# Stick-breaking attention moved from head order to token-tile order, beside the output projection and the FFN

## The chip, the cores and the metric

One core of a Trainium2 chip runs one launch of the kernel. The core has five engines with a queue each: PE (TensorE, matrix multiplication, with its weight loads as PEld), DVE (VectorE), ACT (ScalarE), POOL (GpSimd) and SP, which here issues every DMA. The metric is device time in microseconds (us) of the whole launch; lower is better.

## The reference, cut to what matters

One decoder layer over 2048 positions of width 1024, all in float32:

```python
h = rmsnorm(x, attn_pre_norm)
dq, dk, dv, sq, sk, sv = split(h @ w_qkv)            # 1024 -> 3072
diff_o = rmsnorm(diff_attention(dq, dk, dv))          # 4 heads, two softmax maps of 64, values of 128
# stick-breaking attention, 8 heads of 64, strictly causal
z = sq @ sk.T / 8
log_1mb = where(strict, log_sigmoid(-z), 0)
between = cumsum(log_1mb, reverse) - log_1mb
a = where(strict, exp(log_sigmoid(z) + between), 0)
sb_o = rmsnorm(a @ sv)
x = x + rmsnorm(concat(diff_o, sb_o) @ w_o)
h = rmsnorm(x, ffn_pre_norm)
u = causal_conv3(h @ w_up) + conv_b                   # 1024 -> 2 * 2816
x = x + rmsnorm((gelu(gate) * val) @ w_down)          # 2816 -> 1024
```

## The kernel before, in words

Every float32 operand of a matmul is split into a high part, rounded to the matmul's own type fp32r, and a low part, the rest; each product is three matmuls: high by high, high by low, low by high. So each operand costs a copy ("hi") and a subtraction ("lo") on ACT, DVE or POOL, and PE gets three passes.

The program doesn't run in the order of its loops. Each step of the loops registers its operations with a planner (class `Plan`): engine, estimated cost, dependencies, buffers, and a due time that is the running sum of PE cost in the order of registration (`plan.now`), less a lead. `Plan.run` then plays the operations through, gives each engine at each moment the ready operation that is due first, lets some operations go to either of two engines (`alt`), and writes the instructions out in that order. On the chip each engine works through its own list in order and waits on semaphores. `merge(a, b)` mixes two streams of steps so that both go forward in proportion to their PE cost.

Five kinds of work follow each other, with overlap:

- **QKV.** Five passes over eight blocks of 256 positions (`qkv_steps`, `unit_steps`): 128x256 matmuls into banks `g` (L602, L605), results split and stored to DRAM.
- **Differential attention**, heads 0 to 3 (`diff_stream`), mixed with the passes: logits `z` (L702), softmax on DVE and ACT, 128x128 transposes through PE into banks `t` (L720), a hi copy (L466 or L467) and a lo subtraction (L734), values into bank `o` (L905 to L911).
- **Stick-breaking attention**, heads 4 to 7, two 64-wide maps each (`sb_stream`), after it in head order, 256 positions at a time: per map, per key chunk of up to 512 and per block of 128 queries one `z` (L702), two sigmoids on ACT out of `z` (L969, L971), a running product along the row on DVE (the scan, L977), a product on POOL (L982), then the transposes, hi, lo and two value matmuls (L1000). `fin_sb` normalises, and `mix_out` stores the result. It runs beside the last QKV passes and the first eight blocks of the output projection.
- **Output projection** (`wo_block`, L1101), one block of 128 positions at a time, then residual, second norm and a store of the transposed FFN input (`h2d`).
- **FFN** (`ffn_all`), four tiles of 512 positions: 44 `up` blocks of 24 matmuls (L1226), per block a copy out of PSUM (L1234), two halo copies and three conv operations (L1232, L1235, L1238 to L1240), gelu on ACT (L1243), the product (L1248) and its split (L1249, L1250); then `down` (L1311), two halves of 22 row blocks by four banks. Each weight block (512 KB) is loaded from the input and split again in each of the four tiles (L458, L461, L459). The FFN holds eight PSUM banks.

What sets the due times of attention and FFN is the order at the end of `layer_kernel`:

```python
heads = chain(diff_stream(seq, 32), sb_stream(seq, 32, 2))
...
run(merge(until(heads, *mark), qkv_steps(p, i0, i1)))     # 15 marks
wo_weights()
run(until(heads, 7, 5))
run(merge(until(heads), chain.from_iterable(wo_block(b) for b in range(8))))
for b in range(8, NB):
    run(wo_block(b))
ffn_all()
plan.run()
```

## Time and profile before

| | |
|---|---|
| median of 3 runs | 3088.07 us (3087.9 to 3089.95) |
| the profiled execution, its own time | 3094.23 us |
| span of its instructions | 3092.5 us |
| PE, DVE, ACT, POOL busy in the span | 97%, 73%, 47%, 31% |
| granted TensorE clock, mean | 0.992 of 2.4 GHz |
| instructions on PE (matmul) | 17352 |

The trace holds every instruction with start, duration and tiles. Matmuls are pipelined: one of 512 columns is shown with some 390 ns, while the next starts after some 227 ns. So a busy share of PE is no measure of how densely it is fed; the distance from start to start is. Times in the rows are us from the start of the span, unless ns is said.

### The profile page before, as it was taken

How to read it: one execution, taken by the hardware profiler on the slowest of the kernel's cores; microseconds unless marked ns; L12 is line 12 of the kernel's file. 1: busy time of each engine (PE TensorE's matmuls, PEld its weight loads, DVE VectorE, ACT ScalarE, POOL GpSimd, SP SyncE). 2: the span in 40 equal slices, each digit the busy share in tenths (PEclk: the TensorE clock that was granted, in tenths of full speed). 3: DMA queues.
4: the chain of work that ended last, by engine and by line, in shares of the span. 5: the costliest groups of instructions: out<-in, count | busy, mean ns of one | idle time of the engine just before them, and what ended most of it. 6: DMA issues, size and time to landing. Idle time of an engine off the chain costs nothing. (4 is left out here: it accounts for less than half of the span.)

```text
span 3092.5 us, 48117 instructions
## 1 busy us (share of the span) xinstructions
PE 2984.5 (97%) x17352; PEld 2610.4 (84%) x17352; DVE 2252.0 (73%) x4327; ACT 1442.9 (47%) x2913; POOL 951.6 (31%) x1047
## 2 busy tenths in 40 slices
PE   7999999999999999889999999999999999999998
PEld 7899999999888888868877888888888888888887
DVE  4658878897999999998754864387744776277742
ACT  4434545555777767666643433233322433233321
POOL 1001002002766777675411211033301332023310
PEclk9999999999999999999999999999999999999999
DMA  8776656655634366533363333443344333343332
GB/s 264 246 209 186 185 151 201 171 156 159 188 122 130 95 194 185 151 100 112 110 214 126 102 100 116 121 134 96 96 129 143 96 99 106 119 141 101 96 123 82
DMA packets 392146, 437.11 MB, mean 141 GB/s; under 512 B 20096, under 2 KB 328164, under 8 KB 381668
## 3 DMA queue, kind: packets, MB, share of 16 engines
q1 hardware_dynamic: 391908, 434.05, 46.7%
q8 instruction: 136, 2.23, 0.3%
q14 instruction: 102, 0.84, 0.1%
HBM read 333.30 MB, written 100.67 MB: 140 GB/s over the span
## 5 line engine op out<-in xcount | busy, mean ns | idle before, releaser
L1226 PE MATMUL pu<-fh,fhi 128*128 128x512 f32 x2816 | 869.0, 390 | 0.2 <-ACT fu L1234 0.2
L1226 PEld LDWEIGHTS pu<-fh,fhi 128*128 128x128 f32 x2816 | 529.4, 188 | 110.5 <-ACT fu L1234 0.6
L461 DVE TENSOR_TENSOR flo<-fraw,fhi 128x1024 fp32r<-128x1024 f32 x186 | 233.0, 1254 | 488.6 <-ACT fhi L458 488.5
L1226 PE MATMUL pu<-fh,flo 128*128 128x512 f32 x1408 | 549.2, 390 | 0.0
L982 POOL TENSOR_TENSOR ring_w<-ring_w,ring_a 128x512 f32<-128x512 f32 (+2 forms) x320 | 387.9, 1224 | 220.3 <-DVE ring_a L977 121.1
L605 PE MATMUL g<-hT,big 128*128 128x256 f32 x3072 | 447.8, 288 | 7.3 <-DVE st L638 4.3
L458 ACT CAST fhi<-fraw 128x1024 fp32r<-128x1024 f32 x253 | 265.5, 1051 | 397.4 <-PE py L1311 218.6
L1311 PE MATMUL py<-fhi,gt 128*128 128x512 f32 x1408 | 435.9, 390 | 0.0
L605 PEld LDWEIGHTS g<-hT,big 128*128 128x128 f32 x3072 | 405.4, 192 | 19.8 <-DVE st L638 4.4
L977 DVE TENSOR_TENSOR_SCAN ring_a<-ring_a 128x513 f32<-128x513 f32 (+2 forms) x320 | 412.8, 1316 | 6.1 <-ACT ring_a L969 6.1
L702 PE MATMUL z<-k,q 128*128 128x512 f32 (+3 forms) x1280 | 362.5, 376 | 10.4 <-ACT ring_a L969 7.0
L466 ACT CAST thi<-t 128x512 fp32r<-128x512 f32 (+2 forms) x472 | 221.6, 492 | 210.1 <-PE t L720 179.3
L1311 PEld LDWEIGHTS py<-fhi,gt 128*128 128x128 f32 x1408 | 264.5, 188 | 60.0
L1226 PEld LDWEIGHTS pu<-fh,flo 128*128 128x128 f32 x1408 | 264.7, 188 | 54.9
L734 DVE TENSOR_TENSOR tlo<-t,thi 128x512 fp32r<-128x512 f32 (+2 forms) x528 | 281.6, 556 | 34.6 <-ACT thi L466 28.4
L459 POOL TENSOR_TENSOR flo<-fraw,fhi 128x1024 fp32r<-128x1024 f32 x78 | 195.8, 2510 | 338.9 <-DVE fhi L457 171.2
L1311 PE MATMUL py<-flo,gt 128*128 128x512 f32 x704 | 277.8, 395 | 0.0
L720 PE MATMUL t<-ident,ring_w 128*128 128x128 f32 x1632 | 253.2, 276 | 22.4 <-DVE tlo L734 18.5
L1250 POOL TENSOR_TENSOR gt<-fy,gt 128x512 fp32r<-128x512 f32 x88 | 118.4, 1347 | 493.9 <-ACT gt L1249 483.0
L1239 DVE SCALAR_TENSOR_TENSOR fy<-fu,cw,fy 128x512 f32<-128x512 f32 x176 | 239.6, 1361 | 6.2
L384 POOL TENSOR_TENSOR sm<-sm,neghalf 128x2 f32<-128x2 f32 (+1 forms) x72 | 76.8, 1067 | 536.5 <-DVE sm L382 534.7
L602 PE MATMUL g<-big,hT 128*128 128x256 f32 x1536 | 227.4, 288 | 6.3 <-DVE st L624 1.5
(158 smaller groups left out, 4697.4 us busy)
## 6 DMA issues: line engine op xcount, KB each, us to landing
fraw<-in_w_up_dram SPq DMA_DIRECT2D x176, 512.0 KB, 3.8
hT<-hd SPq DMA_DIRECT2D x64, 1024.0 KB, 7.0
fraw<-in_w_down_dram SPq DMA_DIRECT2D x88, 512.0 KB, 3.8
q<-qd SPq DMA_DIRECT2D x128, 256.0 KB, 4.3
hd<-hT SPq DMA_DIRECT2D x16, 1024.0 KB, 5.4
qd<-st SPq DMA_DIRECT2D x128, 128.0 KB, 2.6
kd<-st SPq DMA_DIRECT2D x128, 128.0 KB, 2.6
vd<-st SPq DMA_DIRECT2D x64, 256.0 KB, 5.2
```

The source lines that it names most:

```text
L458: "ACT", c_act(n) + 42, lambda: nc.scalar.copy(hi(), raw()))
L461: "DVE", c_dvs(n), lambda: nc.vector.tensor_tensor(lo(), raw(), f32(hi()), ALU.subtract))
L602: nc.tensor.matmul(ps.t[:, cs], hk[:, b, c * P:(c + 1) * P], wv[:, a, k, :], start=first, stop=last)
L605: nc.tensor.matmul(ps.t[:, cs], wv[:, a, k, c * P:(c + 1) * P], hk[:, b, :], start=first, stop=last)
L702: nc.tensor.matmul(ps.t[:, 0:w], q.t[:, m, l, jj * P:(jj + 1) * P], kt.t[:, m, 0:w], start=(l == 0), stop=(l == 1 and not masked))
L720: nc.tensor.transpose(ps.t[:, cc * P:(cc + 1) * P], rows[jj].t[:, (k + kk) * P:(k + kk + 1) * P], ident)
L734: ol = op("DVE", c_dvp(n), lambda sl=sl: nc.vector.tensor_tensor(lo.t[:, sl], ps.t[:, sl], f32(hi.t[:, sl]), ALU.subtract), (oh,), (ps, hi ...
L977: nc.vector.tensor_tensor_scan(gr, gr, gr, 1.0 if cb is None else cb[0].t[:, 0:1], ALU.mult, ALU.bypass)
L982: rdeps.append(op("POOL", c_pool(w), lambda be=be, gm=gm, w=w: nc.gpsimd.tensor_tensor(be.t, be.t, gm.t[:, 1:w + 1], ALU.mult), (o1, o2), ...
L1226: nc.tensor.matmul(ps.t, w3(w)[:, k, :], h.t[:, a, k, :], start=(k == 0 and i == 0), stop=(k == KD - 1 and i == 2))
L1239: nc.vector.scalar_tensor_tensor(y.t, u.t[:, 1:TT + 1], cw[:, 1, f:f + 1], y.t, ALU.mult, ALU.add)
L1311: nc.tensor.matmul(ps.t, gt.t[:, a, j * P:(j + 1) * P], wt.t[:, ms], start=(m == 0 and i == 0), stop=(m == NFT - 1 and i == 2))
```

## The change

Nothing of the arithmetic's volume on PE changes. What is done where and when does:

- The planner's matmul cost becomes n * 0.4434 ns, and it knows of a 1300 ns cost when ACT's function changes between `sig` and `gelu` (`table`); it adds that cost to the operation it has picked, and doesn't pick by it.
- Only the four differential heads stay in the first stage, with three and a half of now four QKV passes. Then `sb_open` replaces the left pools, and stick-breaking attention runs by token tiles of 512: tile, then head, map, key chunk from the diagonal down. PSUM: two banks `z2`, one `t2`, one `o2`, and four banks `pf` that projection and FFN share (eight in all).
- The output projection (`wo`) works on a tile of 512. Its input is stored already split (`mixd` holds hi and lo, the norm's gain applied in `mix_out`), and loads straight into matmul operands. The FFN input `h2` is made in SBUF and no longer goes through DRAM.
- Weights are loaded and split once, in pieces of half the size, and the split form is stored to DRAM (`wud`, `wdd`, `wod`); the other three tiles load the split form. Five buffers `W`, in strict order of use.
- FFN in rounds: `up` for 6, 6, 6 and 4 row blocks, each followed by `down` over those, on four banks; partial sums are kept in SBUF (`ya`) and added by DVE.
- The conv takes its first term, scale and bias, on ACT out of PSUM, and two shifted terms on DVE out of PSUM; two short `edge` operations add the halo.

```diff
-    heads = chain(diff_stream(seq, 32), sb_stream(seq, 32, 2))
+    heads = diff_stream(seq, len(seq))
...
-    wo_weights()
-    run(until(heads, 7, 5))
-    run(merge(until(heads), chain.from_iterable(wo_block(b) for b in range(8))))
-    for b in range(8, NB):
-        run(wo_block(b))
-    ffn_all()
+    for mark, p, i0, i1 in (((0, 2), 0, 4, 6), ((0, 4), 0, 6, 8), ((1, 4), 1, 0, 4), ((2, 0), 1, 4, 8),
+                            ((2, 6), 2, 0, 4), ((3, 4), 2, 4, 8), ((), 3, 0, 4)):
         run(merge(until(heads, *mark), qkv_steps(p, i0, i1)))
+    op(None, 0, sb_open, users("k", "v", "q", "thi", "tlo", "mo", "ot", "os", "sq", "mix", "sm", "z", "o", "w", "a"))
+    sb = sb_stream()
+    run(merge(until(sb, 1, 2), qkv_steps(3, 4, 8)))
+    ffn_switch()
+    run(merge(until(sb, 1, 5), wo(0)))
+    run(merge(until(sb, 1, 8), h2(0)))
+    head = list(ffn_head(2))
+    run(merge(until(sb), chain(ffn(0), ffn(1), head[:-5])))
+    run(chain(head[-5:], ffn_tail(2), ffn(3)))
     plan.run()
```

The order inside the FFN, the weights, and the new steps of an `up` block:

```diff
+    ROUNDS = ((0, 6), (6, 12), (12, 18), (18, NFT))
+    def ffn_head(t):
+        for r, (a, b) in enumerate(ROUNDS):
+            for m in range(a, b):
+                for v in range(2):
+                    yield 24 * c_mm(512), lambda m=m, v=v: up(t, m, v)
+            if r + 1 < len(ROUNDS):
+                for h in range(2):
+                    yield from down(t, r, h)
+    def ffn_tail(t):
+        if t + 1 < NTT:
+            yield from wo(t + 1)
+        for h in range(2):
+            yield from down(t, len(ROUNDS) - 1, h)
+        if t + 1 < NTT:
+            yield from h2(t + 1)
...
+    def weight(n):
+        kind, a, b = key = jobs[n]
+        w = buf("W")
+        if key in wstore:
+            wbufs[n] = w, (load(flat, home, 1 << 19, (w,), (wstore[key],), lead=0.0, what="wload"),)
+            return
+        raw = buf("raw2")
...
+        o = load(rv, src, 1 << 18, (raw,), lead=0.0, what="wraw")
+        ds = split(lambda: raw.t, lambda: w.t[:, 0, :], lambda: w.t[:, 1, :], 512, (o,), (raw, w), 0.0)
+        wstore[key] = op(SPE, 0, lambda: nc.sync.dma_start(home, flat()), ds, (w,), 0, 1 << 19, "wstore")
...
+        o1 = op("ACT", c_act(512) + 95, lambda: nc.scalar.activation(
+            y.t, ps.t, AF.Identity, scale=sc(2), bias=sc(3)), (last, *mem["cw"]), (ps, y), what="conv")
+        def conv():
+            nc.vector.scalar_tensor_tensor(y.t[:, 1:TT], ps.t[:, 0:TT - 1], sc(1), y.t[:, 1:TT], ALU.mult, ALU.add)
+            nc.vector.scalar_tensor_tensor(y.t[:, 2:TT], ps.t[:, 0:TT - 2], sc(0), y.t[:, 2:TT], ALU.mult, ALU.add)
...
+            o = op("ACT", 520, lambda: nc.scalar.activation(y.t, y.t, AF.Gelu_apprx_tanh), (o,), (y,)).table("gelu")
```

One unit of the new stick-breaking stream (a map, a key chunk of 512, four query blocks `jj`), its front and one of its four transposing steps:

```diff
+            o = op("PE", 2 * c_mm(w) + (60 if diag else 0), z, [*ql, kl, mem["masks"]], (ps, q, kt), what="z")
+            o1 = op("ACT", c_act(w), lambda: nc.scalar.activation(
+                gm.t[:, 0:w], ps.t[:, 0:w], AF.Sigmoid, scale=-1.0), (o,), (gm, ps), what="sig").table("sig")
+            o2 = op("ACT", c_act(w), lambda: nc.scalar.activation(
+                be.t[:, 0:w], ps.t[:, 0:w], AF.Sigmoid), (o,), (be, ps), what="sig").table("sig")
...
+            o1 = op("DVE", c_scan(w), scan, [o0, o1] + ([cb[1]] if cb else []), [gm] + ([cb[0]] if cb else []),
+                    what="scan")
+            carry[jj] = gm, o1
+            o = op("POOL", c_pool(w), lambda: nc.gpsimd.tensor_tensor(
+                be.t[:, 0:w], be.t[:, 0:w], gm.t[:, 1:w + 1], ALU.mult), (o1, o2), (be, gm), what="mul").alt(
...
+            oh = copy(lambda: hi.t[:, sl], lambda: ps.t[:, sl], n, (o,), (ps, hi), "hi")
+            ol = op("DVE", c_dvp(n), lambda: nc.vector.tensor_tensor(
+                lo.t[:, sl], ps.t[:, sl], f32(hi.t[:, sl]), ALU.subtract), (oh,), (ps, hi, lo), what="lo")
             if pend:
                 av(*pend.popleft())
```

## Rows read from the trace of the kernel before

**Rows 1.** The page, busy time, share of the span, instructions of an engine.

```profile
PE 2984.5 (97%) x17352; PEld 2610.4 (84%) x17352; DVE 2252.0 (73%) x4327; ACT 1442.9 (47%) x2913; POOL 951.6 (31%) x1047
```

**Rows 2.** Busy time of each engine by stretch, clock, DMA share, GB/s.

```profile
core 0: us, PE busy (x) PEld busy (x) DVE busy (x) ACT busy (x) POOL busy (x), PEclk, DMA share, GB/s
0.00:100.00 100.00, 77.89 (x583) 74.21 (x584) 46.67 (x104) 37.77 (x85) 14.60 (x23) 0.97 0.84 267
100.00:800.00 700.00, 690.33 (x5307) 659.60 (x5306) 571.58 (x1859) 354.09 (x809) 85.82 (x110) 1.00 0.63 182
800.00:1500.00 700.00, 640.96 (x4486) 576.03 (x4485) 668.83 (x966) 493.48 (x1137) 488.21 (x686) 0.99 0.46 138
1500.00:1720.00 220.00, 211.69 (x989) 174.25 (x988) 126.59 (x201) 100.25 (x239) 53.20 (x55) 0.98 0.47 154
1720.00:2980.00 1260.00, 1260.00 (x5545) 1041.51 (x5544) 807.45 (x1160) 436.78 (x616) 304.69 (x170) 1.00 0.38 114
2980.00:3092.00 112.00, 103.61 (x453) 84.82 (x451) 30.90 (x40) 20.52 (x31) 5.06 (x5) 0.98 0.27 85
```

**Rows 3.** The chain that ended last, in the FFN: start, us, what.

```profile
2002.97 239.36 PE pu L1226 x1056
2242.33 120.86 PE py L1311 x528
```

**Rows 4.** Timeline in stick-breaking attention, PE alone: start, us, instructions merged.

```profile
1001.61 1.09 PE L702 MATMUL z<-k,q 128*128 128x512 f32 x4
1003.30 0.60 PE L720 MATMUL t<-ident,ring_w 128*128 128x128 f32 x4
1004.44 0.88 PE L602 MATMUL g<-big,hT 128*128 128x256 f32 x6
```

**Rows 5.** Groups of PE by form, whole span: busy, mean ns, idle before.

```profile
L605 PE MATMUL g<-hT,big 128*128 128x256 f32 x3072 | 447.8, 288 | 7.3 <-DVE st L638 4.3 <-DVE st L624 3.0
...
L720 PE MATMUL t<-ident,ring_w 128*128 128x128 f32 x1632 | 253.2, 276 | 22.4 <-DVE tlo L734 18.5 <-DVE ws L382 0.9 <-ACT mo L466 0.7
```

**Rows 6.** Waits of PE in 800 to 1500: us in total, times, longest.

```profile
PE t L720 <- DVE tlo L734: 18.1, 18, 2.7
PE t L763 <- DVE tlo L734: 13.9, 15, 2.0
```

**Rows 7.** Groups of DVE by form, whole span, as in Rows 5.

```profile
L977 DVE TENSOR_TENSOR_SCAN ring_a<-ring_a 128x513 f32<-128x513 f32 x224 | 327.7, 1481 | 4.5 <-ACT ring_a L969 4.5
L1239 DVE SCALAR_TENSOR_TENSOR fy<-fu,cw,fy 128x512 f32<-128x512 f32 x176 | 239.6, 1361 | 6.2
L461 DVE TENSOR_TENSOR flo<-fraw,fhi 128x1024 fp32r<-128x1024 f32 x186 | 233.0, 1254 | 488.6 <-ACT fhi L458 488.5
L734 DVE TENSOR_TENSOR tlo<-t,thi 128x512 fp32r<-128x512 f32 x336 | 223.2, 676 | 29.9 <-ACT thi L466 26.0 <-PE o L911 1.5 <-PE o L1000 1.2
L576 DVE SCALAR_TENSOR_TENSOR hT<-t,g_pre,hT 128x256 fp32r<-128x256 f32 x64 | 27.8, 478 | 23.3 <-ACT hT L574 23.2
L461 DVE TENSOR_TENSOR big<-raw,big 128x512 fp32r<-128x512 f32 x12 | 10.6, 880 | 0.1
```

**Rows 8.** Groups of ACT and POOL by form, whole span, as in Rows 5.

```profile
L466 ACT CAST thi<-t 128x512 fp32r<-128x512 f32 x292 | 171.8, 591 | 149.8 <-PE t L720 127.9 <-PE o L906 5.9 <-DVE ring_w L842 2.5
L969 ACT ACTIVATE ring_a<-z 128x512 f32<-128x512 f32 x224 | 134.7, 608 | 46.7 <-DVE ring_a L977 22.5 <-PE z L702 15.2 <-POOL ring_w L982 2.4
L1243 ACT ACTIVATE fy<-fy 128x512 f32<-128x512 f32 x88 | 55.7, 632 | 251.8 <-DVE fy L1240 251.8
L982 POOL TENSOR_TENSOR ring_w<-ring_w,ring_a 128x512 f32<-128x512 f32 x224 | 302.6, 1360 | 164.7 <-DVE ring_a L977 92.1 <-ACT ring_w L971 27.2 <-PE t L720 14.1
```

**Rows 9.** Timeline of ACT at its third table load: start, us, what.

```profile
1598.63 1.28 ACT L1243 ACT_TABLE_LOAD   x1
1599.93 0.63 ACT L1243 ACTIVATE fy<-fy 128x512 f32<-128x512 f32 x1
```

**Rows 10.** DMA issues: queue, count, KB each, median us from issue to landing.

```profile
fraw<-in_w_up_dram SPq DMA_DIRECT2D x176, 512.0 KB, 3.8
```

More of the change, by code (lines that the diff above doesn't have):

```diff
@@ L73, with table @@
 class Op:
-    __slots__ = ("ways", "eng", "bufs", "prio", "left", "ready", "succ", "start", "end", "nbytes", "what")
+    __slots__ = ("ways", "eng", "bufs", "prio", "left", "ready", "succ", "start", "end", "nbytes", "what", "tab")
+    def table(self, name):
+        self.tab = name
+        return self
     def alt(self, eng, dur, fn):
@@ L235, in run @@
                         fn()
+                        if e == "ACT" and o.tab is not None and o.tab != tab:
+                            tab, dur = o.tab, dur + self.TABLE
                         o.start = t
@@ new lines, in sb_stream @@
+        n, started = 0, -1
+        loads(0)
+        loads(1)
+        for u in range(len(units) + 1):
+            if u < len(units):
+                t = units[u][0]
+                if t != started:
+                    started, n = t, 0
+                yield (t, n), None
+                n += 1
+                if u + 2 < len(units):
+                    yield 0.0, lambda u=u: loads(u + 2)
+                for jj in range(4):
+                    yield 2 * c_mm(512), lambda u=u, jj=jj: front(u, jj)
+            if u:
+                for kb in range(4):
+                    yield 436 + 2 * c_mm(512), lambda u=u, kb=kb: tstep(u - 1, kb)
@@ new lines, in h2, with step, tr @@
+    def h2(t):
+        def step(k):
+            ps, hb = buf("pf"), buf("fh")
+            xs = [x1b[t, j] for j in range(4)]
+            def tr():
+                for j in range(4):
+                    nc.tensor.transpose(ps.t[:, j * P:(j + 1) * P], xs[j].t[:, k * P:(k + 1) * P], ident)
+            o = op("PE", 436, tr, [xdone[t, j] for j in range(4)], (*xs, ps), what="h2T")
+            o1 = op("ACT", c_act(512) + 95, lambda: nc.scalar.activation(
+                hb.t[:, 0, :], ps.t, AF.Identity, scale=g_ffn[:, k:k + 1]), (o, mem["gffn"]), (ps, hb))
+            o2 = op("DVE", c_dvp(512), lambda: nc.vector.scalar_tensor_tensor(
+                hb.t[:, 1, :], ps.t, g_ffn[:, k:k + 1], f32(hb.t[:, 0, :]), ALU.mult, ALU.subtract), (o1,), (ps, hb))
+            h2b[t][k] = hb, (o1, o2)
+        for k in range(KD):
+            yield 436, lambda k=k: step(k)
@@ new lines, in down, with part, go, evac @@
+    def down(t, r, h):
+        a, b = ROUNDS[r]
+        st = {}
+        def part(i, js):
+            m = a + i
+            if m not in st:
+                st[m] = take("d", m, h)
+            w, wd = st[m]
+            gt, g1, g2 = gts[t, m]
+            for j in js:
+                if i == 0:
+                    st["ps", j] = buf("pf")
+                ps = st["ps", j]
+                def go(j=j, ps=ps):
+                    for n, (x, y) in enumerate(((0, 0), (0, 1), (1, 0))):
+                        nc.tensor.matmul(ps.t, gt.t[:, x, j * P:(j + 1) * P], w.t[:, y, :],
+                                         start=(i == 0 and n == 0), stop=(m == b - 1 and n == 2))
+                prev = st.get(("last", j))
+                st["last", j] = op("PE", 3 * c_mm(512), go, [g1, g2, *wd] + ([prev] if prev else []), (w, gt, ps),
+                                   what="dn")
+                if m == b - 1:
+                    evac(j, ps, st["last", j])
+        def evac(j, ps, last):
+            if r == 0:
+                y = buf("ya")
+                yas[t, h, j] = y, copy(lambda: y.t, lambda: ps.t, 512, (last,), (ps, y))
+                return
+            y, o = yas[t, h, j]
+            o = op("DVE", c_dvp(512), lambda: nc.vector.tensor_tensor(y.t, ps.t, y.t, ALU.add), (last, o), (ps, y))
+            yas[t, h, j] = y, o
+            if r < len(ROUNDS) - 1:
+                return
@@ L1320, in ffn_all @@
[L1320 to L1339 removed]
+            rb = 4 * t + j
```

712 lines of the change are left out of this document (330 added, 382 removed), and 6 rows, old and new, of tables (heads, tag).

## The prediction

> **What bounds the kernel now.** I read the busy shares first [rows 1]: PE at 97% looks like a kernel with nothing left. But a matmul is shown longer than it holds the next one up, so I took the distances from start to start. In the FFN 1056 matmuls of 512 columns pass in 239.36 us, 226.7 ns each, and 528 of `down` in 120.86 us, 228.9 ns [rows 3]. In attention four transposes take 0.60 us, and the last is shown for some 0.27, so (0.60 - 0.27) / 3 = 109 ns; likewise 228 ns for a `z` matmul of 512 and 117 ns for one of 256 [rows 4]. With 172 and 60 ns for 384 and 128 columns (in proportion; they are few) I add up the 31 groups of PE, of which [rows 5] shows two: QKV 4608 x 117 = 539 us, `z` and masks 256, transposes 241, value matmuls 223, projection 768 x 227 = 174, `up` 4224 x 226.7 = 957, `down` 2112 x 228.9 = 483: **2873 us** of dense feeding. The span is 3092.5 us, so **220 us** are lost.
>
> The same sum by stretch, on the counts of [rows 2], says where: 0 to 100 holds 67 us of feeding (33 lost), 100 to 800 holds 659 (41 lost, 6.2% on top), 800 to 1500 holds 582 (**118 lost**), 1500 to 1720 203 (17 lost), 1720 to 2980 1258 (2 lost), the rest 102 (10 lost). The worst stretch is stick-breaking attention: there DVE is busy 668.83 of 700 us, ACT 493, POOL 488, while in the FFN behind it DVE has 807 of 1260 and ACT 437 [rows 2]. What PE waits for there is DVE's lo subtraction [rows 6]; only 59 us of the 118 show as idle, the rest are matmuls that come late one by one. So: a stage at DVE's limit, followed by one where PE runs dense and DVE has a third of its time free.
>
> **The change, part by part.** *PE's own work* stays. The same columns of `z`, transposes, values, projection, `up` and `down` are issued; value matmuls become 512 wide instead of 256, with the same sum of columns (227 against 2 x 117 ns, 3 us less in all). Feeding is 2869 us, the sum of the five stages below. The gain can only come out of the 220. I cut the new order into five stages, with PE feeding by the distances above.
>
> *Stage A*, differential attention with 3.5 QKV passes: 307 + 0.875 x 539 = 779 us. Start as before, 33 lost. The rest, 712, at the 6.2% of 100 to 800, which is the same mixture: 44 lost. DVE gets more room there, as half a pass more of PE work lies beside it; between 3% and 6.2% I stay with the row.
>
> *Stage B*, the second half of the last pass beside ten stick-breaking units: a diagonal unit is 3.6 us of PE, a full one 5.4 (8 `z` x 227, 16 transposes x 109, 8 values x 227), so 67 + 44 = 111 us. `sb_open` waits until every buffer of the first stage is done, but QKV keeps PE fed meanwhile; 7 at 6.2% and some 5 for loads and the first chain of sigmoid, scan, product: 12 lost.
>
> *Stage C*, projection of tile 0, six units, `h2`: 76 us. Here `ffn_switch` waits for the last QKV store, and behind it stand the first raw weights: a load (3.8 us for twice the size [rows 10]), hi and lo, some 6 us with only stick-breaking to feed PE. Then the chain projection, norm, residual, store of `x1` (which the scaling waits for, being in place), transposes: some 12 us against three units' cover. In 1500 to 1720, the like passage of before, 17 were lost; I take 19.
>
> *Stage D*, the core: 64 units (44 full, 20 diagonal) beside tiles 0 and 1 and most of tile 2. PE: 127 `up` x 24 x 226.7 = 691, `down` 1488 x 228.9 = 340, two projections 87, `h2` 7, stick-breaking 309 + 13: 1447 us. Is another engine the limit in it? DVE: a full unit has four scans at 1481 and four lo at 676 ns [rows 7] = 8.6 us, a diagonal one 6.2, together 503 with 34 for the norms on top. An `up` block has two terms of conv out of PSUM: between the 676 ns of L734 and twice the 478 of a 256 column operation of that form (L576) I take 725 each, 184 in all; were the first term as slow as L1239, whose mean is 1361, and the second 956 [rows 7], 294. L734 has one input in PSUM as these have, and none of that lengthening, so I stay near it. Edges 33, gate product 47, `ya` sums 64 x 0.69 = 44, norms and `h2` 53, half of tile 0's weight lo 66 x 880 ns = 58. Sum 956 to 1066 of some 1490: 64 to 72%. ACT: a full unit 8 sigmoids x 608 and 4 hi x 591 [rows 8] = 7.2 us, with the diagonal ones and norms 460; conv, halo, gelu (632), casts, squares 250; weight hi 83: 793. POOL: 44 x 4 x 1360 [rows 8] = 239, others 290: 36%. None reaches PE's time. What goes with it: three of four tiles no longer split weights, 198 of 264 blocks, each 1254 ns of DVE (or more of POOL) and a hi on ACT; `halo` and `fu` copies shrink. All of that was hidden behind PE in 1720 to 2980 [rows 2], so it gives no time by itself; it makes the room that stick-breaking goes into.
>
> *Table loads.* Gelu and sigmoid now alternate on ACT. Before there were three table loads in all; a switch costs 1.28 us, and the gelu starts 20 ns behind its end [rows 9]. At most two per gelu: 63 x 2 x 1.283 = 162 us, ACT 955 of 1490 (64%). Hidden, as long as nobody waits for ACT at that moment; the hi copy out of the only `t2` bank does (a rival, below). The Trainium skill speaks against this part ("ScalarE: Activation LUTs", What ACT_TABLE_LOAD costs, and its rule to group functions by table set): it gives some 2.66 us per switch, load and drain. The trace shows the load and no drain behind it. By the skill's figure ACT would have some 1128 us, still below PE, so the sum stays, and the rival would be dearer.
>
> What is lost in D: between the 0.1% of 1720 to 2980 and the 6.2% of 100 to 800, where DVE was busier (82%). I give the 322 us of stick-breaking 6.2% (20), and the FFN's 1125 some 2%, for single `t2`, four shared `pf` banks and a planner that rates DVE's operations some 10% short: together **40**, with 2 and 90 as ends.
>
> *Stage E*, five `up`, the last projection, last round of tile 2, `h2`, tile 3: 456 us of FFN alone. New joints: the projection's input needs the `fh` buffers of the last `up`, a DMA of 3.8 us [rows 10] with 4.1 us of that block left as cover (2 lost, 4 without it); `h2` goes through four banks at some 0.7 us per bank and engine (3); rounds need their last bank copied out, some 2 us after the last matmul, with three other banks as cover (2 in all). 9 with the row's 2. The end: 10 before; one more sum and a product behind the last bank, 12.
>
> *DMAs.* All on SP. Tile 0 loads 38.8 MB raw, stores 77.6 MB split, and has some 29 MB of other traffic in stages C and D's first third, some 571 us: 254 GB/s. The first 100 us moved 267 GB/s at a share of 0.84 [rows 2]. So it just fits; that is the second rival. Later tiles need 512 KB per 12 matmuls (2.72 us), 193 GB/s at most; five buffers give 13.6 us for a landing of 3.8. The store of a split piece stands on SP behind its split, and later loads behind that; the raw loads run ten pieces ahead. Value stores are two DMAs instead of one, 64 more issues in 850 us, hidden.
>
> **Sum.** 2869 + 33 + 44 + 12 + 19 + 40 + 9 + 12 = 3038 us of span. The profiled execution took 1.7 us more than its span (3094.23 against 3092.5), and the median lies 6.2 below that execution; 3038 + 1.7 - 6.2 = **3033 us**, 1.8% faster.
>
> **The rivals.** *The FFN takes it in without a trace:* D and A as dense as they can be (2 and 21 lost): 3033 - 38 - 23 = 2972, with half of it 2990. For: DVE at 64 to 72%. Against: 100 to 800 has an in-order PE behind ACT and DVE and loses 6.2%, most of it within PE's busy time (41 lost, 10 idle). Chance 0.14.
>
> *DMA limits tile 0.* If the mixture moves only the 226 GB/s that the second 100 us show at a 0.72 share, 145 MB take 642 instead of 571 us; with half of it hidden by what waits anyway: some +40, 3073. For: small raw packets, and a `W` buffer is held until its store has landed. Against: 254 is below 267. Chance 0.13.
>
> *ACT becomes the clock of stick-breaking (slower).* Place: stage D, the hi copy out of the single `t2`. Before it stands, in each gelu's case, load, gelu, load: 3.2 us. No transpose can start in that time, and PE's list is fixed, so it waits with `up` work behind it. With 1.5 us of wait per gelu, 63 x 1.5 = 95: 3128 us. It decides from 55 / 63 = 0.87 us per gelu, where the gain is gone. For: one bank where before had two `t`. Against: a step has 1487 / 256 = 5.8 us on average, and its own chain is some 2.2. Chance 0.11. By the skill's 2.66 us it would be 63 x 2.8 more.
>
> *The spreading doesn't happen*, stick-breaking bunches at the start of D and leaves DVE at its limit there: the 118 of before come back, 3033 + 80 = 3113. Against: the merge is by PE cost. Chance 0.03.
>
> **How the numbers follow.** Forecast 0.59, round 3005 to 3065. The ends: down to 2985 (half the first rival), up to 3090 (D at its upper end, or DMA); what lies outside is the slow rivals and the best case, some 0.2. About 0.2%, 6 us, is what a measurement of this kernel tells from nothing. Faster: 0.56 of the forecast's 0.59, 0.14, and 0.11 of DMA's 0.13: 0.81; within 0.2% the other 0.03 and 0.02: 0.05; slower 0.11 + 0.03 = 0.14.
>
> **What would show it.** Right: the stretch with sigmoids in it is some 1500 us long with DVE at 60 to 75%; PE's waits for lo are short and many; no stretch has DVE over 90%. Table loads: some 60 to 126. Wrong: a DMA share above 0.85 in tile 0 with PE waiting for a DMA; or PE's longest waits name ACT's hi behind table loads; or gaps of over 5 us at `sb_open`, `ffn_switch` and each `h2`.

## The result

The change made the kernel **slower by 6.2%**: 3282.93 us median of four runs (3278.06 to 3286.75) against 3089.01 of the kernel before (four runs, 3087.9 to 3095.66), a ratio of 1.0622 with a 95% interval of 1.0601 to 1.0644. The forecast was 3033 (2985 to 3090): wrong in its sign, and outside its range.

The profiled execution took 3278.06 us, its span 3276.3. The stages below are cut where the matmuls change (first `z` of stick-breaking, last QKV, first projection, first and last `up` of each tile). The table answers [rows 2]: busy time of each engine by stretch, then PE's granted clock, the DMA share and the GB/s, kernel after.

```profile
core 0: us, PE busy (x) PEld busy (x) DVE busy (x) ACT busy (x) POOL busy (x), PEclk, DMA share, GB/s
0.00:100.00 100.00, 79.28 (x586) 75.81 (x587) 45.13 (x99) 37.24 (x83) 14.40 (x23) 0.95 0.80 259
100.00:877.00 777.00, 765.22 (x5936) 734.41 (x5935) 561.22 (x1870) 352.48 (x786) 67.03 (x70) 1.00 0.64 191
877.00:993.00 116.00, 103.29 (x716) 94.83 (x714) 82.72 (x155) 53.11 (x135) 42.28 (x76) 0.93 0.61 176
993.00:1042.00 49.00, 35.82 (x131) 23.64 (x130) 33.54 (x49) 24.63 (x54) 17.62 (x23) 0.76 0.67 208
1042.00:1166.00 124.00, 98.28 (x410) 75.48 (x411) 81.79 (x125) 50.08 (x110) 41.09 (x57) 0.83 0.64 214
1166.00:1666.00 500.00, 454.08 (x2053) 358.26 (x2052) 358.47 (x473) 242.97 (x438) 172.74 (x191) 0.98 0.66 218
1666.00:1789.00 123.00, 106.78 (x482) 83.26 (x481) 84.82 (x125) 52.46 (x114) 36.31 (x49) 0.95 0.65 223
1789.00:2251.00 462.00, 447.18 (x2096) 363.95 (x2095) 314.25 (x478) 216.70 (x369) 86.77 (x138) 0.99 0.56 182
2251.00:2360.00 109.00, 99.80 (x469) 79.17 (x467) 76.48 (x120) 48.18 (x103) 29.22 (x44) 0.98 0.65 220
2360.00:2805.00 445.00, 439.40 (x2076) 358.44 (x2077) 299.67 (x455) 201.40 (x351) 79.18 (x124) 1.00 0.56 180
2805.00:2892.00 87.00, 73.04 (x320) 59.12 (x319) 37.65 (x69) 22.45 (x51) 12.18 (x15) 0.94 0.75 261
2892.00:3253.00 361.00, 360.40 (x1585) 296.74 (x1584) 130.69 (x253) 71.70 (x110) 2.20 (x3) 1.00 0.61 192
3253.00:3276.00 23.00, 0.21 (x1) 0.00 (x0) 13.13 (x19) 1.44 (x4) 6.58 (x6) 0.60 0.53 160
```

With the prediction's own distances (227 ns for a 512 column matmul, 109 for a transpose) PE's dense feeding is 2868.8 us, as it reckoned (2869). So the whole miss lies in what is **lost beside the feeding**, 407.5 us instead of 169. (The expectations below name some losses 1 to 3 us higher, such as 178 for D and 53 for C: there the transposes of `h2` stand at 60 ns instead of 109.)

| stage of the prediction | stretch, us | forecast lost | lost | lost in the mended kernel (below) |
|---|---|---|---|---|
| first 100 us | 0 to 100 | 33 | 32 | 29 |
| A | 100 to 877 | 44 | 45 | 28 |
| B | 877 to 993 | 12 | 31 | 17 |
| C: switch; projection of tile 0, `h2` | 993 to 1042; to 1166 | 19 | 30 + 51 | 17 + 31 |
| D: `up` and `down` of tile 0 | 1166 to 1666 | | 79 | 13 |
| D: joint, tile 1, joint, tile 2 | 1666 to 2805 | | 30 + 32 + 17 + 17 | 12 + 9 + 12 + 8 |
| D, sum | | 40 | 175 | 54 |
| E: joint and tile 3 | 2805 to 3253 | 9 | 19 + 2 | 18 + 0 |
| the end | 3253 to 3276 | 12 | 23 | 18 |

(For instance 1166 to 1666: 2051 matmuls and transposes by those distances are 421.1 us of 500.) Tile 3, alone, is as dense as the FFN of the kernel before: rounds on four banks cost nothing. What was built on top of it costs: where stick-breaking, weight splits and FFN meet, PE loses 16% (tile 0) and 24% (the joint behind it), and **on the average of tile 0 no engine is near its limit**: DVE has 358 of 500 us, ACT 243, POOL 173, DMA a share of 0.66. Such an average hides peaks: of the 82 pieces of 20 us from 1166 to 2806 nine have DVE busy over 90%, and they hold 42 of the 175 us lost in D. The other 133 are lost where DVE is busy less than that.

PE's waits from 877 to 1789 in the kernel after (us in total, times, longest) answer [rows 6]:

```profile
PE t L1027 <- DVE lo L1034: 19.1, 31, 2.2
PE o L1050 <- ACT hi L482: 12.1, 27, 1.0
PE z L995 <- ACT be L1003: 11.4, 24, 1.7
PE t L1027 <- DVE os L1072: 8.9, 8, 3.6
```

Many short waits, each for the last step of a chain that goes through DVE or ACT. That is the picture that the prediction had called right; it holds, and the time is lost all the same. As I read it, each engine, following its list, waits a little for another that isn't late by much.

### The profile page after: what moved, and what is told of

It is laid out like the page before. It is cut to its first block, busy times and chain, and to the rows that moved or that the text cites. A ratio compares the mean times of both kernels' runs of the same rounds, so it can differ in the third digit from the quotient of the medians.

```text
span 3276.3 us, 46690 instructions
## 1 busy us (share of the span) xinstructions
PE 3062.8 (93%) x16840; PEld 2603.1 (79%) x16840; DVE 2119.6 (65%) x4280; ACT 1374.8 (42%) x2702; POOL 607.6 (19%) x817
## 4 chain that ended last, share of the span: by engine, by line
PE 70%; DVE 16%; ACT 5%; issue 3%; DMA 1%; POOL 1%; SPq 0%; POOLq 0%; DVEq 0%; ACTq 0%
PE pf L1292 21%; PE pf L1345 13%; PE g L620 9%; PE g L617 5%; PE pf L1212 5%; DVE gm L1009 4%; PE t L1027 3%; PE z L723 3%; PE z L995 2%; PE o L1050 2%; PE t L741 2%; DVE lo L1034 1%; DVE fy L1303 1%; DVE fy L1304 1%; PE o L903 1%
## 5 line engine op out<-in xcount | busy, mean ns | idle before, releaser
L1292 PE MATMUL pf<-fh,W 128*128 128x512 f32 x4224 | 1045.9, 396 | 5.4 <-DVE W L477 2.5
L1292 PEld LDWEIGHTS pf<-fh,W 128*128 128x128 f32 x4224 | 789.8, 189 | 173.2 <-DVE W L477 4.2
L1345 PE MATMUL pf<-W,gt 128*128 128x512 f32 x2112 | 531.6, 396 | 10.4 <-ACT junk L1230 4.2
L1345 PEld LDWEIGHTS pf<-W,gt 128*128 128x128 f32 x2112 | 392.2, 189 | 98.8 <-ACT junk L1230 6.1
L1013 POOL TENSOR_TENSOR be<-be,gm 128x512 f32<-128x512 f32 (+3 forms) x216 | 261.1, 1212 | 887.2 <-ACT be L1003 606.7
L1009 DVE TENSOR_TENSOR_SCAN gm<-gm,gm 128x513 f32<-128x513 f32 x192 | 278.2, 1471 | 58.3 <-ACT gm L1001 56.9
L1303 DVE SCALAR_TENSOR_TENSOR fy<-pf,cw,fy 128x511 f32<-128x511 f32 x176 | 131.0, 744 | 265.7 <-ACT fy L1299 213.0
L1034 DVE TENSOR_TENSOR lo<-t,hi 128x512 fp32r<-128x512 f32 (+1 forms) x320 | 193.2, 604 | 121.1 <-ACT hi L482 118.4
L1027 PE MATMUL t<-ident,be 128*128 128x128 f32 x1088 | 187.5, 290 | 49.1 <-DVE lo L1034 28.0
L617 PEld LDWEIGHTS g<-big,hT 128*128 128x128 f32 x1536 | 210.7, 197 | 9.9 <-ACT big L474 1.7
L1212 PE MATMUL pf<-W,fh 128*128 128x512 f32 x768 | 188.6, 401 | 6.3 <-POOL W L475 3.5
```

The lines of the kernel that those rows point to most:

```text
L617: nc.tensor.matmul(ps.t[:, cs], hk[:, b, c * P:(c + 1) * P], wv[:, a, k, :], start=first, stop=last)
L1009: nc.vector.tensor_tensor_scan(gr, gr, gr, 1.0 if cb is None else cb[0].t[:, 0:1], ALU.mult, ALU.bypass)
L1013: o = op("POOL", c_pool(w), lambda: nc.gpsimd.tensor_tensor(be.t[:, 0:w], be.t[:, 0:w], gm.t[:, 1:w + 1], ALU.mult), (o1, o2), (be, gm), w ...
L1027: nc.tensor.transpose(ps.t[:, jj * P:(jj + 1) * P], rows[jj][0].t[:, kb * P:(kb + 1) * P], ident)
L1034: ol = op("DVE", c_dvp(n), lambda: nc.vector.tensor_tensor(lo.t[:, sl], ps.t[:, sl], f32(hi.t[:, sl]), ALU.subtract), (oh,), (ps, hi, lo), ...
L1212: nc.tensor.matmul(ps.t, mb.t[:, a, j * P:(j + 1) * P], w.t[:, b, :], start=(k == 0 and n == 0), stop=(k == KD - 1 and n == 2))
```

## Experiments: bank, weights, mixture, tables

Four theories stood against each other. B: the single `t2` bank. W: the way of tile 0's weights (load, split, store, five `W` buffers). M: stick-breaking is late since DVE and ACT are. T: the table loads, the prediction's slow rival.

**One bank moved from `z2` to `t2`.**

```diff
-("z2", 2), ("o2", 1), ("pf", 4)
+("z2", 1), ("o2", 1), ("pf", 4)
-T["t2"] = Tag(1, fifo=False, bank=True)
+T["t2"] = Tag(2, fifo=False, bank=True)
```

> One of the two z2 banks of stick-breaking goes to the transposes: z2 has 1 bank, t2 has 2, everything else as in the changed kernel (3283 us). Theory B (the single t2 bank is what the losses hang on: a transpose waits for hi and lo of the step before): about half of the 170 us lost in stages B, C and the first tile go, 3190 to 3220, and PE's wait for the lo subtraction ahead of transposes (28 us in the changed kernel) falls below 10. Theory W (tile 0 is paced by its weight pieces: load, split, store, five W buffers): nothing but the 20 to 30 us of stages B and C, where there are no weights, 3250 to 3270, and PE's loss from 1210 to 1800 us stays over 100. Theory M (stick-breaking is late because DVE and ACT are late, whatever the banks): 3275 to 3290.

3243.06 us, ratio 1.0495 (1.0459 to 1.0531): 40 us better. That lies between the ranges of B and W. Stage B lost 21 instead of 31, the switch 19 instead of 30, C 45 instead of 51, tile 1 23 instead of 32, tile 0 still 74. PE's waits from 876 to 1757 in this kernel:

```profile
PE z L995 <- ACT be L1003: 35.6, 47, 2.0
PE o L1050 <- DVE lo L1034: 11.0, 23, 1.6
```

The transposes' wait for lo has left the head of the list; now a `z` waits for the sigmoid that frees its only bank. B is a part of the loss, the smaller one. Tile 0's was hardly touched.

**Weights not kept:** no piece is stored, each tile splits its own again.

```diff
-wstore[key] = op(SPE, 0, lambda: nc.sync.dma_start(home, flat()), ds, (w,), 0, 1 << 19, "wstore")
```

> Undoes one part, weights split once: no piece is stored, every tile loads raw weights and splits them again as before the change, in the changed kernel's order otherwise. It takes 132 stores of 512 KB (wud, wdd) and 16 (wod) out of tile 0, turns 512 KB loads of tiles 1 to 3 into 256 KB ones, and adds 3 x 148 pieces of hi and lo on ACT, DVE and POOL. Theory W: the 121 us lost from 1210 to 1800 us fall to 50 or less, some 20 more in the projection of tile 0; tiles 1 to 3 lose no more than 30 us through the added splits: 3180 to 3230. Theory M (DVE's load in the mixture makes PE late): tile 0 changes by less than 20 us, and the added splits, some 440 x 1.3 us of DVE and POOL work, make tiles 1 and 2 lose 50 or more: 3310 to 3350. Theory B: tile 0 unchanged, 3280 to 3300.

3265.13 us, ratio 1.0567 (1.0532 to 1.0601): only 18 better, but two large movements cancel. Tile 0's loss fell from 79 to 38 and C's from 51 to 28, as W had it; tiles 1 and 2 with the joint between them, which split again, went from 66 to 122. So keeping the split weights is worth some 56 us there, and storing them, in this order, costs some 64 in tile 0 and C (whether by bytes, by the queue or by the planner's reckoning, the runs below tell). That the removal of the splits "gives no time by itself" was wrong: beside stick-breaking it does. Tile 3, alone, lost 1 to 2 us with them or without.

**No stick-breaking in stage D.**

```diff
-units = [(t, g, m, c) for t in range(NTT) ... for c in range(t, -1, -1)]
+units = [(t, g, m, c) for t in range(NTT) ... for c in range(t, -1, -1)][:16]
```

> Leaves out the stick-breaking attention behind its first 16 units, that is all 64 units of stage D (tiles 2 and 3, and the diagonal and full units behind unit 16; the projections of the later tiles take other heads' mixes in place of the missing ones). 320 us of PE feeding, all of the sigmoids, scans and lo copies of stage D go; the FFN with its weight splits and stores stays. Theory W: tile 0's FFN loses at least as much as before, as it is now shorter and its weights are not: its 44 up tiles and down rounds, some 349 us of feeding, take 450 us or more; the total is 3283 - 320 - some 50 = 2900 to 2950. Theory M or B: the FFN without stick-breaking beside it feeds as densely as in the kernel before, 355 us for tile 0; total 3283 - 320 - 150 = 2800 to 2830.

2921.55 us, within W's range for the whole, though tile 0 took 433 us and not the 450 or more that W named. Tile 0's FFN, alone on the chip now, loses **95 us**; tiles 1, 2 and 3 lose 1, 0 and 2. So tile 0 is late through its weights, without any stick-breaking. The timelines of this kernel show how. SP's queue first (start, us, what):

```profile
1394.82 4.59 SPq L1171 DMA_DIRECT2D wud<-W  x4
1399.47 10.66 SPq L392 DMA_DIRECT2D raw<-in_w_up_dram  x4
1410.18 4.58 SPq L1171 DMA_DIRECT2D wud<-W  x4
1414.81 12.51 SPq L392 DMA_DIRECT2D raw<-in_w_up_dram  x4
```

Four stores (L1171), then four raw loads (L392), then four stores, in a beat of some 15 us. PE's timeline in the same time:

```profile
1391.64 13.76 PE L1292 MATMUL pf<-fh,W 128*128 128x512 f32 x60
1408.43 14.17 PE L1292 MATMUL pf<-fh,W 128*128 128x512 f32 x48 [3.03 <-ACT W L474]
```

PE stands 3 us for the hi copy of a piece whose raw load came behind the stores. And the wait is paid twice: the 48 matmuls behind it take 14.17 us, 295 ns each, because the first 12 run at the lower clock (1408.43 to 1414.22, most at 427 ns instead of 227). The stretches of this kernel show it: tile 0 from 1300 on, tile 1, and the 4 us behind that wait (columns as above):

```profile
1300.00:1587.00 287.00, 245.50 (x928) 189.55 (x926) 117.72 (x158) 81.29 (x156) 16.65 (x13) 0.89 0.61 213
1682.00:2021.00 339.00, 338.85 (x1491) 279.88 (x1490) 120.48 (x233) 70.23 (x137) 1.30 (x1) 1.00 0.61 200
1408.00:1412.00 4.00, 3.42 (x7) 2.32 (x8) 2.54 (x3) 1.42 (x3) 1.28 (x1) 0.50 0.24 73
```

A granted clock of 0.50 is the level of 1.2 GHz; tile 0 has 0.89 from 1300 on, tile 1 has 1.00. (The Trainium skill, "TensorE: Matmul & The Clock Gate", Part 1, gives 426.7 ns for a 512 column matmul at the lower clock; the trace agrees.) And DMA, with a share of 0.61, isn't full: it is badly timed.

**No table loads:** gelu is replaced by a sigmoid.

```diff
-AF.Gelu_apprx_tanh), (o,), (y,)).table("gelu")
+AF.Sigmoid), (o,), (y,)).table("sig")
```

> Gelu is replaced by a sigmoid (the FFN's activation is another one; all else stays), so that ACT never changes its table in stage D: 114 table loads of 1.28 us, 146 us of ACT, go. Theory T (the slow rival of the prediction: transposes wait for hi behind load, gelu, load): 3283 - 95 or more, 3190 or less. Theories W, M and B: ACT is 47% busy and nobody waits for it long, 3268 to 3288.

3265.09 us, ratio 1.0566 (1.0526 to 1.0606): 18 better, between the two expectations and near the second. The kernel after has 114 loads in this part (60 to 126 were forecast), 146 us of ACT. Its timeline of ACT (start, us, what) answers [rows 9]:

```profile
1458.42 1.28 ACT L1315 ACT_TABLE_LOAD   x1 [0.26 <-DVE fy L1304]
1459.71 0.63 ACT L1315 ACTIVATE fy<-fy 128x512 f32<-128x512 f32 x1
```

The function starts 10 to 20 ns behind the load. (The Trainium skill, "ScalarE: Activation LUTs", What ACT_TABLE_LOAD costs, has the same 1283 ns and a drain of some 1380 ns on top; no such drain shows here.) The edit takes the planner's 1300 ns per switch out as well, so the 18 us, most of them in tile 1 (21 lost instead of 32), are the loads and the order written for them together: 0.12 us for each of the 146 us of ACT. The rival is real and small.

## Experiments: the end, DVE's splits, the stores' queue, the planner's costs

**The last residual loaded whole,** into the idle `x1` buffers.

```diff
-yc, xb = yas[t, c, j][0], buf("xr")
+if t == NTT - 1: big = buf("x1"); lx = load(lambda: big.t, x1d[rb], 1 << 19, (big,), ...)
```

> The last tile's residual is loaded whole (512 KB) into the four x1 buffers, which are idle by then, in place of halves through the two xr buffers. Theory on the end: the 23 us behind the last matmul of the changed kernel are loads of xr that wait one for another; they fall to 9 to 12 as in the kernel before, 3283 - 12 = 3271. If the end is the chain of sum, norm, product and store by itself, it stays at 20 or more: 3280 to 3286.

3280.15 us, ratio 1.0615 (1.0584 to 1.0646): nothing in the whole. At the end itself it worked by half: the chain that ended last in the kernel after (start, us, what) has two loads one behind the other for want of an `xr` buffer,

```profile
3261.87 1.68 POOL ya L1381
3263.57 4.06 DMA xr<-x1d
3267.72 0.70 DVE ya L1383
3268.43 4.19 DMA xr<-x1d
3272.72 0.69 DVE ya L1383
```

and without them the stretch from the last matmul to the end is 16 instead of 23 us (8.8 in the kernel before). But in the profiled execution tile 0 lost 86 instead of 79, although the lists of DVE and ACT are the same up to the last operations: so far do two executions of one order differ (3278.06 to 3286.75 for the kernel after), and a gain of 7 us can't be seen in the whole.

**Tile 0's splits on ACT and POOL alone.**

```diff
 def split(raw, hi, lo, n, deps, bufs, lead):
+    if T["pf"].made:    # hi on ACT, lo on POOL, no choice
```

> The pieces of FFN and projection weights of tile 0 are split on ACT (hi) and POOL (lo) alone; in the changed kernel DVE takes 81 of the lo and some 30 of the hi. Stores stay. Theory D (DVE is what backs up in tile 0): some 95 us of DVE leave a stretch of 570 us, and tile 0's loss of 79 us falls below 50: 3240 to 3260. Theory W (the way of the pieces through SP's queue, raw buffers and stores): a piece gets ready no sooner, as POOL's lo takes 1.5 us against DVE's 0.9; 3275 to 3300.

3255.6 us, ratio 1.0536 (1.0501 to 1.0571): 27 better; tile 0 lost 51 instead of 79, near theory D's 50, the rest much as before. That fits a DVE that backs up in tile 0: busy 72% on average, over 90% in three of its 25 pieces of 20 us. The edit changes the order too, so it doesn't show it alone.

**Stores issued by ACT.**

```diff
-wstore[key] = op(SPE, 0, lambda: nc.sync.dma_start(home, flat()), ds, (w,), 0, 1 << 19, "wstore")
+wstore[key] = op("ACT", 60, lambda: nc.scalar.dma_start(home, flat()), ds, (w,), 0, 1 << 19, "wstore")
```

> The stores of split pieces are issued by ACT instead of SP; bytes, buffers and loads are the same, but the order in which the kernel's planner issues work can change with it. Theory W1 (order on SP's queue: a store stands there behind its split, and the next raw loads behind the store): tile 0's loss falls from 79 to about 40 and stage C's from 53 to 30, as in the kernel without stores, while tiles 1 and 2 keep their 33 and 17: 3283 - 64 = 3219, up to 3240. Theory W2 (bytes: a W buffer is held until its 512 KB have landed, or the DMA engines are full): tile 0 loses 70 or more as now, 3270 to 3290.

3208.77 us, ratio 1.0384 (1.0354 to 1.0414): 74 better; tile 0 lost 35, C 36, the joint 21. As W1 had it, and 10 us below its range, bytes unchanged. But the edit has a second effect, as an operation of ACT it is no longer charged to the planner's reckoning of DMA, and that was to matter.

**Measured costs in the planner.** Groups of DVE by form in the kernel after (busy, mean ns, idle before):

```profile
L1009 DVE TENSOR_TENSOR_SCAN gm<-gm,gm 128x513 f32<-128x513 f32 x192 | 278.2, 1471 | 58.3 <-ACT gm L1001 56.9 <-POOL gm L999 0.8
L1034 DVE TENSOR_TENSOR lo<-t,hi 128x512 fp32r<-128x512 f32 x224 | 153.3, 684 | 109.2 <-ACT hi L482 107.2
L1303 DVE SCALAR_TENSOR_TENSOR fy<-pf,cw,fy 128x511 f32<-128x511 f32 x176 | 131.0, 744 | 265.7 <-ACT fy L1299 213.0 <-ACT halo L1312 52.2
L1304 DVE SCALAR_TENSOR_TENSOR fy<-pf,cw,fy 128x510 f32<-128x510 f32 x176 | 131.8, 749 | 6.2
L477 DVE TENSOR_TENSOR W<-raw,W 128x512 fp32r<-128x512 f32 x81 | 73.5, 913 | 16.5 <-ACT W L474 16.1
L1015 DVE TENSOR_TENSOR be<-be,gm 128x512 f32<-128x512 f32 x77 | 65.3, 851 | 10.5 <-ACT be L1003 8.0 <-DVE gm L1009 0.5
L1309 DVE SCALAR_TENSOR_TENSOR fy<-halo,cw,fy 128x1 f32<-128x1 f32 x132 | 41.4, 314 | 4.7
```

```diff
 c_act:  52 + n / 1.2       ->  149 + 0.871 * n
 c_dvp:  68 + 1.043 * n     ->  150 + 1.047 * n
 c_dvs:  130 + 1.043 * n    ->  283 + 1.043 * n
 c_scan: 130 + 2.083 * n    ->  200 + 2.45 * n
 c_copy: 68 + 0.5215 * n    ->  360 + 0.5215 * n
 c_pool: 148 + 2.1 * n      ->  330 + 2.1 * n
 conv 2 * 620 -> 2 * 747; edge 260 -> 543; conv on ACT + 95 -> + 180; gelu, gt 520 -> 633, 621
```

The planner has 1197 for the scan's 1471, 602 for lo's 684, 1240 for the two conv terms' 1493, 664 for the 851 and 913 of L1015 and L477, 260 for the two edge operations' 543. (Part of the excess of L1009, L1015 and L477 comes and goes with POOL's work beside them; see the last section.)

> The planner's cost of each kind of DVE, ACT and POOL operation is set to what the trace of the changed kernel shows (scan of 512 columns 1454 instead of 1197 ns, PSUM operand 686 instead of 602, two SBUF inputs 817 instead of 664, both conv terms 1494 instead of 1240, edge 543 instead of 260, sigmoid 595 instead of 479, conv on ACT 775 instead of 574, POOL product 1405 instead of 1223); it only changes the order of the work and which engine takes it. Theory P (the order is wrong since the planner rates these engines 10 to 40% too fast, so that PE's list puts matmuls ahead of data that isn't there yet): losses of stage D's 178 and of B and C fall by a third, 3283 - 90 = 3190 to 3230. Theory W and B (buffers, banks and queue): 3265 to 3295.

3179.09 us, ratio 1.0288 (1.0258 to 1.0318): **104 better**, more than theory P hoped for, with the same operations as before (only ACT's table loads went from 115 to 127, and some splits and products moved from DVE to POOL). Tile 0 lost 36, tiles 1 and 2 10 each. The kernel carried out an order in which these operations were thought shorter than they are (they take 14 to 109% more); as I read it, every list then has operations ahead of their data on the chip, and what stands behind them waits too. The run itself shows that the order and the choice of engines alone were worth 104 us.

## Experiments: what adds up, and the planner's DMA rate

> Four edits together: measured costs in the planner (3179 by itself), stores of split pieces issued by ACT (3209), one z2 and two t2 banks (3243), the last residual loaded whole (3280). If the losses are separate (queue order, bank, order of work), the gains of 104, 74, 40 and 3 us add up: 3062. If costs and stores cure the same thing, tile 0's loss (79 us, 36 with the costs, 35 with the stores), the stores give only what is left of it, some 20 to 30, and the bank some 20 of stages B and C: 3120 to 3140. It beats the kernel before (3090) only in the first case.

Costs, stores on ACT, `t2` bank and end together: 3108.48 us, ratio 1.006 (1.0042 to 1.0078), 174 better, 47 short of the sum of the single gains (221), between the two expectations, and not below the kernel before. The edits are the four diffs above.

> Measured costs and stores issued by ACT, without the other two edits. Separate losses: 3283 - 104 - 74 = 3105. One loss cured by either: 3179 less 10 to 25, 3155 to 3170.

Costs and stores on ACT: 3141.85 us, 1.0168 (1.0146 to 1.019). 141 of 178, so the two overlap by 37: tile 0's loss is 18, where each alone left 35. What happens is between the two expectations.

> The kernel before the change with the same measured costs of its planner (all forms that the two kernels share; its conv, which is priced by a figure of its own, is left). If the wrong costs are a fault that both kernels carry, the kernel before gains as well, above all in its stick-breaking stage (118 us lost, DVE at its limit): 3040 to 3070, and the change stays slower by the same 100 us. If they hurt only where FFN and stick-breaking share engines, 3080 to 3095.

The same diff of the cost functions in the kernel before: 3117.54 us, 1.0089 (1.0068 to 1.0111), 27 **slower**. Neither expectation. So it isn't true that every order gains by measured costs: in the old order, where stick-breaking ends at DVE's limit and the FFN runs behind it, these figures did harm. Why is open. They were taken from the other kernel, and the old conv kept its 2036 ns, which fits the medians of its three operations (L1238 to L1240, 2046 in all) and not their means (2843).

**One number.** The planner reckons DMAs as a single line at 250 GB/s:

```diff
-dma = max(dma, t + 1600) + o.nbytes / 250.0
+dma = max(dma, t + 1600) + o.nbytes / 300.0
```

> The changed kernel with one number of its planner changed: the rate at which it reckons DMA, 250 to 300 GB/s, so that in tile 0 a raw load and a store (768 KB) are reckoned at 2.6 us, less than the 2.7 us that PE needs per piece. Stores stay on SP. Theory W1 (the order on SP's queue itself makes the raw loads late): tile 0 keeps its loss of 79 us or gets worse, 3265 to 3300. Theory W3 (the planner thinks that DMA paces tile 0 and writes PE's and SP's lists for that, and the stores on ACT's queue helped as it no longer charges them): tile 0's loss falls to 40 or less as with the stores on ACT, 3200 to 3230.

3178.24 us, ratio 1.0282 (1.0261 to 1.0302): **105 better**, 22 more than W3 hoped for, with every store still on SP. Tile 0 lost 35 instead of 79, C 36, B 19. W1 falls, W3 stands: not SP's queue as such, but an order written for DMAs that were thought too slow. A piece of tile 0 (256 KB in, 512 KB out) is reckoned at 3.1 us at 250 GB/s, while PE needs 2.72 for it; so by its reckoning tile 0 is bound by DMA, and on the chip each engine keeps to the order written for that. SP's own waits in tile 0 show the turn. Kernel after, 1166 to 1666 (us in total, times, longest):

```profile
SPq L1171 <- DVE W L477: 72.8, 36, 5.7
SPq L392 <- POOL W L475: 54.3, 16, 6.5
SPq L392 <- DVE W L477: 43.1, 10, 11.7
...
SPq L1171 <- POOL W L475: 35.4, 21, 4.8
```

With the rate at 300, 1116 to 1581:

```profile
SPq L392 <- DVE W L477: 121.3, 50, 14.7
SPq L392 <- POOL W L475: 67.4, 29, 6.2
...
SPq L1171 <- DVE W L477: 11.8, 10, 2.4
SPq L1171 <- POOL W L475: 8.0, 5, 2.5
```

Before, stores (L1171) stood 108 us at the head of SP's queue for a split that wasn't done, with raw loads behind them. With the new rate that is 20 us, and the loads (L392) wait for a raw buffer to come free: the weights are ahead of PE as far as three buffers let them.

> The four edits that together gave 3108 us, with the planner's DMA rate at 300 GB/s and one more W buffer in place of a gt buffer. In the 3108 us kernel tile 0 still loses 14 us, the other two up stretches 9 each, the joints 16 to 20 each. If the order of SP's loads still costs something there and in the first stage (36 us lost), 3070 to 3095, below the kernel before (3090); if what is left are chains of norm, transposes and evictions at the joints, 3100 to 3110.

```diff
-("gt", 7), ("W", 5), o.nbytes / 250.0
+("gt", 6), ("W", 6), o.nbytes / 300.0
```

With these on top of the four edits: 3087.28 us, 0.9985 (0.9975 to 0.9995).

> The same kernel with the stores left on SP. Theory W3: with a DMA rate that fits, the queue that issues the stores makes no difference, within 10 us of the kernel with stores on ACT. Theory W1: 30 us or more slower than that, tile 0's loss over 35.

The same with the stores back on SP: **3082.76 us, 0.9969 (0.9958 to 0.9979)**, 200 better than the change and 0.3% better than the kernel before. With these numbers SP is no worse a place for the stores. Stretches of this kernel, B with the switch, C, tile 0, joint (columns as above):

```profile
857.00:995.00 138.00, 122.16 (x848) 108.80 (x848) 107.37 (x191) 80.98 (x200) 50.53 (x101) 0.96 0.75 223
995.00:1093.00 98.00, 82.05 (x368) 63.61 (x367) 70.76 (x101) 49.45 (x108) 42.14 (x58) 0.90 0.79 269
1093.00:1530.00 437.00, 434.67 (x2078) 357.34 (x2077) 338.01 (x464) 258.48 (x458) 175.80 (x197) 1.00 0.75 254
1530.00:1636.00 106.00, 101.80 (x492) 82.84 (x490) 81.73 (x128) 53.12 (x116) 31.89 (x48) 0.95 0.77 262
```

In tile 0 PE loses only 13 of 437 us (clock 1.00) while DMA moves 254 GB/s and DVE has 338 of 437 us.

> The changed kernel with the planner's numbers alone mended: measured costs and the DMA rate of 300 GB/s; banks, buffers, queues and the end as they are. If the two numbers cure the same losses, 3140 to 3165 (each alone gave 3179); if they are separate, 3283 - 104 - 105 = 3075; the kernel with bank, buffer and end mended as well took 3083.

Costs and rate alone, all else as in the change: 3112.06 us, 1.0069 (1.0048 to 1.009). 171 of 209, between the two expectations: the planner's figures alone carry most of the loss, and the two corrections overlap by 38. D loses 66 instead of 175. (No rate but 250 and 300 was tried.)

> The 3083 us kernel without the measured costs: DMA rate, second t2 bank, W buffer and the end only. If the costs matter beside a right DMA rate, it is 30 or more slower, 3110 to 3140; if they only stood in for the rate, 3080 to 3095.

The 3083 us kernel without the measured costs: 3141.41 us, 1.0164 (1.014 to 1.0189), 59 slower. The costs don't merely stand in for the rate.

> The kernel before the change with its planner's DMA rate at 300 GB/s, nothing else. If the low rate is a fault that only the changed tile 0 feels (raw load and store of each piece), the kernel before stays within 10 us of its 3090. If every order written under it is late, it gains 20 to 40 us, in the first stage (41 us lost from 100 to 800 us) above all, as the changed kernel's first stage did by 11, and the version that now beats 3090 does not beat it.

The kernel before with the rate at 300: 3083.87 us, 0.9977 (0.9968 to 0.9987), 6 better: little, as the first expectation had it, but the second one's last clause holds as well. The mended change and the kernel before with this one number mended can't be told apart (3082.76 and 3083.87). So no gain of the spreading by token tiles over the old order was measured, though the old order's buffers and banks were not gone through as the new one's were.

## Why the prediction was wrong

- **PE's own work** (2869): right, 2868.8. **First 100 us and A** (33, 44): right, 32 and 45.
- **Rounds on four banks, FFN alone** (9 for E): E measured 20, but tile 3 itself lost 2; the joint ahead of it took 19, half of it gaps in `h2`, which waits for the scaled rows. The step took the FFN's density from [rows 2] rightly and costed the chain of norm, store and scaling too low.
- **D, 40 us: the step that failed.** It measured 175. The single terms of the shares were near: scans 1481 and 1471 ns, the conv terms 725 and 744 to 749, 114 table loads of at most 126. But the work fell to other engines: DVE did 1134 us from 1166 to 2805 where 956 to 1066 were forecast, as the planner gave it 126 hi copies (79 us) and 85 products (69 us) that the forecast had on ACT and POOL. The share of 69% agrees with the forecast's 64 to 72% only since D took 1639 us instead of some 1490; ACT had 762 us instead of 955, 46% instead of 64%. From "none reaches PE's time" the prediction took that little is lost, and gave a flat 2% of the FFN's 1125 us for, among others, "a planner that rates DVE's operations some 10% short". That term was mis-sized, in two ways. DVE's operations take 14 to 109% more than the planner's figures, not 10; measured costs for DVE, ACT and POOL together gave 104 us by themselves, 72 of them in D. (Its own rows said more than 10: the scan took 1481 ns [rows 7] where the planner has 1197, 24% more.) And the planner's DMA rate was not looked at: the prediction worked out that tile 0 needs 254 GB/s and held it against the 267 of [rows 2], while the planner holds it against 250. The rate alone gave 105 us, 60 of them in D. Both together took D from 175 to 66.
- **DMA limits tile 0** (0.13, 3073): wrong as put; the mended kernel moves 254 GB/s in tile 0 at a share of 0.75 with PE dense, just the rate that the sum called for. The planner's belief that DMA bounds tile 0 was worth 44 of the 79 us lost there, and its wrong costs, cured alone, 43.
- **ACT and the table loads** (0.11, 3128): the right sign and a small part, 18 us. The single `t2` bank that it named cost 40 by another way: the next transposes wait for lo, not for a gelu.
- **B and C** (12 and 19): measured 31 and 81. The cover of the switch by stick-breaking alone was reckoned as if a unit took its PE time, while in 993 to 1042 PE got 19 us of feeding in 49; mean granted clocks of 0.76 and 0.83 add to it. The mended kernel still loses 65 there.
- **The end** (12): 23. The two `xr` buffers were not counted; without them it was 16.
- The signs that should have shown it came in part or not at all: a DMA share of 0.66 in tile 0 instead of over 0.85, DVE over 90% only in pieces of 20 us, and of the gaps over 5 us at the joints one, 5.1 us in the last `h2`. 175 us were lost in D with no more of them than that.
- Two slips decided nothing: half of the first rival's 61 us gives 3002 and not 2990, and the second 100 us of the kernel before moved 224 GB/s, not 226.

In the mended kernel D loses 54 and the whole span 212.3: the forecast's 40 for D was near what the new structure can do with other figures in its planner, a second `t2` bank and a sixth `W` buffer, not what this kernel does. B, C, the joints and the end remain at 125 of those 212.3; what would bring them down was not tried.

## What to carry to other kernels

Where a program writes each engine's list ahead, its cost figures are part of the kernel: compare each with the trace, the DMA rate too, before believing that work fits beside other work, and all the more where the new mixture comes within some per cent of a figure. Busy shares far from 100% say that an order without loss may exist, not that the written one is it. Look at what the DMA queue waits for: loads that wait for free buffers are ahead of the work, stores that wait for their producers are behind it.
